# A retuned gather schedule: 0.62 instead of 0.8 row gathers per block during the routing, and the last rows spread to four blocks from the end

## The chip, the cores and the metric

The kernel runs on one core of a Trainium2 chip. The metric is the device time of one execution in microseconds (us); the time of the kernel before is the median of three runs.

## The reference, cut to what matters

One encoder layer: a hyena branch and an RG-LRU branch, mixed into h, then a PEER layer and a final norm. The change lies in the PEER layer, which looks 16,384 single-neuron experts up by product keys and sums the chosen ones:

```
q = (x @ wq).reshape(B, L, PEER_HEADS, 2, D_HALF)
s = jnp.einsum('blhpd,hpkd->blhpk', q, keys)
ts, ti = lax.top_k(s, K)                       # 16 of 128 keys, twice
cs, ci = lax.top_k((ts[..., 0, :, None] + ts[..., 1, None, :]).reshape(...), K)
experts = e1 * N_KEYS + e2                     # 8 heads x 16 experts a token
g = softmax(cs)
act = gelu(einsum('td,tkd->tk', xt, u_tab[et])) * gt
out = einsum('tk,tkd->td', act, v_tab[et])
```

There are 512 tokens, D = 1024, and two expert tables u and v of 16,384 x 1024 float32.

## The kernel before

The PEER layer treats the 512 tokens in two ways. For the first 384 tokens (TD) nothing is gathered: all 128 **blocks** of 128 experts are multiplied through. A u block is 24 matmuls (ps_e) of the block's weights with x2, followed by a gelu on ScalarE (L1019); a v block is 18 matmuls into ob (L1045) with the weights pt = gelu x routing weight. For the last 128 tokens (TG) the rows themselves are gathered from the tables by indirect DMAs that GpSimd issues (L1160), 512 KB each (128 tokens, one row of 4 KB each): 128 gathers from u, each followed by a dot product on VectorE (L1194, called a *dot* below), then 128 from v, each followed by an accumulation on VectorE (L1215).

Every block's weights come as float32 by a DMA on SyncE's queue (wf, L149) and are split into two float16 halves, the high one on ScalarE (L119), the low one on VectorE (L120); four such wh buffers exist, so the splits can run about two blocks ahead of TensorE.

The order of the work is written by one loop over `seq`: 101 u blocks, then 27 pairs of a u and a v block, then v blocks (in the code i counts v blocks, 0 to 127). The instructions of each engine run in the order in which the loop writes them. Three sources feed VectorE:

- the split of the block two ahead;
- until the routing is done, `pull` draws background steps (the **routing**: selecting the experts, and for the 384 tokens building one-hot tiles oh and og, which TensorE multiplies into ps_gt and ScalarE copies to stg, L1369). `pull` adds PACE = 4.2 us of nominal VectorE time a block to a budget and draws steps until it is spent;
- `gathers(rate)`: adds `rate` to a credit gcr and runs one gather step (a dot, or later an accumulation, and the issue of the gather five rows on) for each whole credit. During the routing each step takes 1.3 us from the same budget.

There are 264 gather steps, the last five being `gather_end`: it adds the residual to acc2 by two TensorE results (ps_x, L1224 and L1227) and runs `final` for the last 128 tokens. When the routing is done, the block in which that happens flushes the remaining ps_gt, closes the routing's PSUM pool and opens the one for ob; from then on `gathers` runs at GRATE[1] = 1.5 a block, and from v block i = 32 at a rate that spreads what is left. The last VT = 3 v blocks are held back and multiplied per 128 tokens just before `final`.

The gather steps in the routing and the stages after it:

```
self.pull(*self.PACE)
self.bud[0] -= 1.3 * gathers(self.GRATE[0])
```

Of the kernel before, what the change touches and what calls it, by code (L numbers as in the profile page):

```python
# [66 lines left out]
class Kernel:  # L67
# [813 lines left out]
    def peer(self, acc):  # L881
        nc, tc, a = self.nc, self.tc, self.a
        E0, LV, VT = self.E0, self.LV, self.VT
# [93 lines left out]
        def gload(k, q):  # L977
            if k < 128 // EB:
                b = order[EB * k] // EB
                if b not in gin:  # L980
                    gin[b] = vp.tile([128, NCH, EB, CH], F32, name="gin", bufs=2)
                cs = slice(q * NCH // 4, (q + 1) * NCH // 4)
                nc.sync.dma_start(gin[b][:, cs].rearrange("p c e t -> p c (e t)"),
                                  gd[cs, :, CH * EB * b:CH * EB * (b + 1)].rearrange("c p n -> p c n"))
# [7 lines left out]
        def pmul(i):  # L992
            if i >= 128:
                return
            e = order[i]
            if i % EB in (3, 5, 7, 9):
                gload(i // EB + 1, (i % EB - 3) // 2)
            sload(i + 6)
            f = pf[i] = vp.tile([128, TD], F32, name="pf", bufs=2)
            nc.vector.tensor_tensor(f.rearrange("p (c t) -> p c t", c=NCH),  # L1000
                                    sin[e // 2][:, e % 2, :].rearrange("p (c t) -> p c t", c=NCH),
                                    gin[e // EB][:, :, e % EB, :], OP.mult)

        def phi(i):
            if i < 128:
                pt[i] = vp.tile([128, 2, TD], F16, name="pt", bufs=4)
                nc.scalar.activation(pt[i][:, 0, :], pf[i], AF.Copy)  # L1007

        def plo(i):
            if i < 128:  # L1010
                nc.vector.tensor_tensor(pt[i][:, 1, :], pf.pop(i), pt[i][:, 0, :], OP.subtract)  # L1011

        def gelu(e, ps):
            if e % 2 == 0:
                gs[0] = xp.tile([128, 2, TD], F32, name="gs", bufs=3) if e < E0 else \
                    vp.tile([128, 2, TD], F32, name="hs", tag="sin", bufs=4)
                if e >= E0:
                    sin[e // 2] = gs[0]
            nc.scalar.activation(gs[0][:, e % 2, :], ps[:, :TD], AF.Gelu_apprx_tanh, scale=1.0 / (S_N * S_W))  # L1019
            if e % 2 == 1 and e < E0:  # L1020
                self.dq.append((sd[e // 2], gs[0]))

        def spill():
            while self.dq:
                nc.sync.dma_start(*self.dq.pop(0))  # L1025

        def gathers(rate):
            if self.gidx is None:
                return 0
            self.gcr = min(self.gcr + rate, 2.0)  # L1030
            n = 0
            while self.gcr >= 1.0 and self.gq:
                self.gstep()
                self.gcr -= 1.0
                n += 1
            return n
# [3 lines left out]
        def vmm(tt, w, pp, first, last):  # L1040
            mm = nc.tensor.matmul
            sl = slice(tt * 128, tt * 128 + 128)
            for k, (x, y) in enumerate(((0, 0), (0, 1), (1, 0))):
                for h in range(2):
                    mm(ob[tt][:, h, :], pp[:, x, sl], w[:, y, h * 512:(h + 1) * 512],  # L1045
                       start=first and k == 0, stop=last and k == 2)
# [7 lines left out]
        rate = None  # L1054
        for pos, (kind, e) in enumerate(seq):
            if kind == "u":
                w = self.w_get(u0 + pos)
                spill()
                ps = ups.tile([128, 512], F32, name="ps_e", tag="s", bufs=utag)
                for c in range(8):  # L1060
                    self.mm3(ps[:, :TD], w[:, 0, c * 128:(c + 1) * 128], w[:, 1, c * 128:(c + 1) * 128],
                             x2[:, 0, c, :TD], x2[:, 1, c, :TD], c == 0, c == 7)
                if prev is not None:
                    gelu(*prev)
                prev = (e, ps)
                if vp is None:
                    self.pull(*self.PACE)
                    self.bud[0] -= 1.3 * gathers(self.GRATE[0])
                else:
                    gathers(self.GRATE[1])  # L1070
                if vp is None and (route not in self.bgq or e == E0 - 3):
                    while route in self.bgq:
                        self.pull(1.0, 1.0)
                    gelu(*prev)
                    prev = None
                    spill()
                    rctx.close()
                    sctx.close()
                    vp = ctx.enter_context(tc.tile_pool(name="vp", bufs=1, side="right"))
                    self.po = ups = ctx.enter_context(tc.tile_pool(name="pso", bufs=1, space=PSUM))  # L1080
                    utag = 2
                    ob += [ups.tile([128, 2, 512], F32, name="ob%d" % k, tag="ob%d" % k) for k in range(3)]
                    gload(0, 0)
                    e0 = e
                elif vp is not None and e in (e0 + 1, e0 + 2, e0 + 3):
                    gload(0, e - e0)
                    if e == e0 + 1:
                        nc.vector.tensor_scalar(self.ident, self.ident, S_P * S_V, None, op0=OP.mult)
                continue
            i, vi = vi, vi + 1  # L1090
            if i == 0:
                for k in range(3):
                    pmul(k)
                    if k < 2:
                        phi(k)
                        plo(k)
            phi(i + 2)
            pmul(i + 3)
            if i >= 128 - E0:
                if rate is None:  # L1100
                    rate = (268 - self.gsteps) / (E0 - 5.0)
                gathers(rate)
            else:
                gathers(self.GRATE[1])
            plo(i + 2)
            w = self.w_get(u0 + pos)
            pp = pt.pop(i)
            if i >= 128 - VT:
                wl.append((w, pp))
                continue  # L1110
            for tt in range(3):
                vmm(tt, w, pp, i == 0, False)
            if prev is not None:
                gelu(*prev)
                prev = None
            k = i - (128 - E0) - 20
            if 0 <= k < 24:
                tt, c = divmod(k, 8)
                nc.tensor.matmul(ob[tt][:, c // 4, c % 4 * 128:c % 4 * 128 + 128],  # L1119
                                 acc[:, c, tt * 128:tt * 128 + 128], self.ident,  # L1120
                                 start=False, stop=False, skip_group_check=True)
# [23 lines left out]
    E0 = 96  # L1145
    LV = 5
    PACE = (4.2, 4.2)
    TB = 8
    GRATE = (0.8, 1.5)
    LAG = 2  # L1150
    GB = 6

# [388 lines left out]
```

## Time and profile before

| what | value |
|---|---|
| median of 3 runs | 1673.27 us (1672.91 to 1676.97) |
| the profiled execution's own time | 1672.62 us |
| its span | 1670.8 us, so 1.8 us lie around the span |
| TensorE busy | 1610.5 us (96%) |
| VectorE busy | 1407.0 us (84%) |
| ScalarE busy | 767.9 us (46%) |
| GpSimd busy | 379.6 us (23%) |
| DMA | 435.06 MB, mean 260 GB/s |

The shares are means over stages with different limits. The stages that matter here, by the start of the span: the u blocks begin at 578 us, the routing's part with gathers lies between about 690 and 1002 us, u blocks alone follow to 1052 us, pairs to 1256 us, v blocks alone to 1664 us.

### The profile page before, as it was taken

How to read it: one execution, taken by the hardware profiler on the slowest of the kernel's cores; microseconds unless marked ns; L12 is line 12 of the kernel's file. 1: busy time of each engine (PE TensorE's matmuls, PEld its weight loads, DVE VectorE, ACT ScalarE, POOL GpSimd, SP SyncE). 2: the span in 40 equal slices, each digit the busy share in tenths (PEclk: the TensorE clock that was granted, in tenths of full speed). 3: DMA queues.
4: the chain of work that ended last, by engine and by line, in shares of the span. 5: the costliest groups of instructions: out<-in, count | busy, mean ns of one | idle time of the engine just before them, and what ended most of it. 6: DMA issues, size and time to landing. Idle time of an engine off the chain costs nothing. (4 is left out here: it accounts for less than half of the span.)

```text
span 1670.8 us, 25107 instructions
## 1 busy us (share of the span) xinstructions
PE 1610.5 (96%) x9451; PEld 901.7 (54%) x9451; DVE 1407.0 (84%) x2422; ACT 767.9 (46%) x1055; POOL 379.6 (23%) x357
## 2 busy tenths in 40 slices
PE   7999999899989988999998999999999999999998
PEld 5675666444435554666665665555554445544443
DVE  7736679987756799899999996998889998899975
ACT  5424278984431333444755763433333333333343
POOL 0000000002200000332222223555455333333400
PEclk9999999999999999999999999999999999999999
DMA  5342141229932246887888999999999999999951
GB/s 199 96 155 76 38 140 64 65 69 323 338 137 76 77 135 196 301 289 263 308 321 308 340 359 394 406 401 372 380 376 372 398 398 401 394 370 402 398 209 71
DMA packets 137738, 435.06 MB, mean 260 GB/s; under 512 B 13040, under 2 KB 37872, under 8 KB 134160
## 3 DMA queue, kind: packets, MB, share of 16 engines
q1 hardware_dynamic: 95360, 279.72, 46.4%
q0 software_dynamic: 42256, 153.73, 24.4%
q8 instruction: 74, 1.21, 0.3%
q14 instruction: 48, 0.39, 0.1%
HBM read 377.83 MB, written 55.57 MB: 259 GB/s over the span
## 5 line engine op out<-in xcount | busy, mean ns | idle before, releaser
L1045 PE MATMUL ob<-wh,pt 128*128 128x512 f16 x2304 | 505.9, 379 | 0.9 <-ACT pt L1007 0.9
L120 DVE SCALAR_TENSOR_TENSOR wh<-wf,wh 128x1024 f16<-128x1024 f32 (+1 forms) x324 | 389.8, 1207 | 96.8 <-ACT wh L119 96.5
L119 ACT ACTIVATE wh<-wf 128x1024 f16<-128x1024 f32 (+1 forms) x324 | 336.0, 1039 | 107.4 <-DMA wf<-in_peer_u 35.9
L1045 PEld LDWEIGHTS <-pt 128*128 128x128 f16 x2304 | 225.4, 98 | 264.3 <-ACT pt L1007 1.3
L126 PE MATMUL ps_e<-x,wh 128*128 128x384 f16 x1024 | 335.4, 328 | 16.3 <-DVE wh L120 16.3
L124 PE MATMUL ps_e<-x,wh 128*128 128x384 f16 x1024 | 335.1, 327 | 3.3 <-ACT gs L1019 2.3
L125 PE MATMUL ps_e<-x,wh 128*128 128x384 f16 x1024 | 335.4, 328 | 0.0
L1160 POOL DMA_INDIRECT rows<-in_peer_un,gidx x128 | 190.6, 1489 | 358.9 <-DVE junk L1194 314.8
L1160 POOL DMA_INDIRECT rows<-in_peer_v,gidx x128 | 163.2, 1275 | 235.3 <-DVE acc L1215 211.4
L126 PEld LDWEIGHTS <-wh 128*128 128x128 f16 x1376 | 135.1, 98 | 137.1 <-DVE wh L120 29.4
L125 PEld LDWEIGHTS <-wh 128*128 128x128 f16 x1376 | 135.1, 98 | 110.0 <-issue 6.3
L124 PEld LDWEIGHTS <-wh 128*128 128x128 f16 x1376 | 135.2, 98 | 104.0 <-issue 2.1
L1007 ACT ACTIVATE pt<-pf 128x384 f16<-128x384 f32 x128 | 66.8, 522 | 246.1 <-issue 217.7
L1215 DVE SCALAR_TENSOR_TENSOR acc<-rows,dots,acc 128x1024 f32<-128x1024 f32 x127 | 162.6, 1280 | 0.9
L1194 DVE SCALAR_TENSOR_TENSOR junk<-rows,xn 128x1024 f32<-128x1024 f32 x128 | 156.0, 1219 | 0.9
L331 PE MATMUL ps_p<-n,wh 128*128 128x264 f16 x960 | 112.5, 278 | 1.6 <-DVE wh L120 1.5
L1019 ACT ACTIVATE gs<-ps_e 128x384 f32<-128x384 f32 x96 | 47.0, 489 | 138.2 <-PE ps_e L126 126.1
L331 PEld LDWEIGHTS <-wh 128*128 128x128 f16 x960 | 94.4, 99 | 20.4 <-issue 3.5
L1369 ACT ACTIVATE stg<-ps_gt 128x512 f32<-128x512 f32 x96 | 93.0, 1079 | 19.8 <-PE ps_gt L1362 14.3
L1011 DVE TENSOR_TENSOR pt<-pf,pt 128x384 f16<-128x384 f32 x128 | 71.5, 559 | 12.8 <-ACT pt L1007 11.8
L124 PE MATMUL ps_p<-n,wh 128*128 128x512 f16 x192 | 73.6, 383 | 0.0
L125 PE MATMUL ps_p<-n,wh 128*128 128x512 f16 x192 | 73.4, 382 | 0.0
(288 smaller groups left out, 1922.7 us busy)
## 6 DMA issues: line engine op xcount, KB each, us to landing
wf<-in_peer_u SPq DMA_DIRECT2D x128, 512.0 KB, 5.9
wf<-in_peer_v SPq DMA_DIRECT2D x128, 512.0 KB, 10.6
gd<-stg SPq DMA_DIRECT2D x24, 1024.0 KB, 9.2
gin<-gd SPq DMA_DIRECT2D x32, 768.0 KB, 15.1
wf<-in_w_in SPq DMA_DIRECT2D x44, 512.0 KB, 3.6
sd<-gs SPq DMA_DIRECT2D x48, 384.0 KB, 7.1
sin<-sd SPq DMA_DIRECT2D x48, 384.0 KB, 12.6
pre<-ph POOLq DMA_DIRECT2D x18, 512.0 KB, 5.6
```

The source lines that it names most:

```text
L119: self.nc.scalar.activation(hi, src, AF.Copy, scale=s)
L120: self.nc.vector.scalar_tensor_tensor(lo, src, s, hi, op0=OP.mult, op1=OP.subtract)
L124: mm(ps, lh, rh, start=first, stop=False)
L125: mm(ps, lh, rl, start=False, stop=False)
L126: mm(ps, ll, rh, start=False, stop=last)
L331: nc.tensor.matmul(ps[:, h, :HL], x, n[:, y, c, h * HL:(h + 1) * HL], start=(c == 0 and x is lh and y == 0), stop=(c == 7 and x is ll))
L1011: nc.vector.tensor_tensor(pt[i][:, 1, :], pf.pop(i), pt[i][:, 0, :], OP.subtract)
L1045: mm(ob[tt][:, h, :], pp[:, x, sl], w[:, y, h * 512:(h + 1) * 512], start=first and k == 0, stop=last and k == 2)
L1160: self.nc.gpsimd.indirect_dma_start(out=r, out_offset=None, in_=table, in_offset=bass.IndirectOffsetOnAxis(ap=self.gidx[:, j:j + 1], axis=0))
L1194: nc.vector.scalar_tensor_tensor(junk, rows.pop(0), 1.0, self.xn, op0=OP.mult, op1=OP.mult, accum_out=self.dots[:, j:j + 1])
L1215: nc.vector.scalar_tensor_tensor(acc2, r, d, acc2, op0=OP.mult, op1=OP.add)
L1369: nc.scalar.activation(st[c][:, :, o:o + 4].rearrange("p e t -> p t e"), ps, AF.Copy, scale=S_P / S_G)
```

## The change

Two numbers. GRATE[0], the gather steps admitted per block during the routing, goes from 0.8 to 0.62; the rate of the last part is worked out so that the 264 steps end four blocks later.

```diff
@@ peer
             if i >= 128 - E0:
                 if rate is None:
-                    rate = (268 - self.gsteps) / (E0 - 5.0)
+                    rate = (263 - self.gsteps) / (E0 - 4.0)
                 gathers(rate)
@@ class Kernel
-    GRATE = (0.8, 1.5)
+    GRATE = (0.62, 1.5)
```

Because a gather step takes 1.3 us of the budget from which the routing is drawn, fewer steps let the routing be drawn faster: counted in the programs, the block in which the routing ends is the 86th u block instead of the 90th. Up to the routing's last og VectorE has 36 dots instead of 51 and 64 splits instead of 69, counted from the point where the gathers' indices (gidx) are made. At the third set of transposes ps_r (end of the last selection) TensorE has done 71 u blocks instead of 74, and VectorE has run 26 dots instead of 37 and 139 splits instead of 142, with the same 26 og. At v block 32 the accumulations done are 15 instead of 24; from there to v block 96 they are 78 instead of 77. No instruction is added or removed over the whole program.

VectorE where the routing ends, before (oh and og are the routing's one-hot tiles, junk the dot, wh the split):

```order
L1384 TENSOR_TENSOR oh<-iota,ed 128x2048
L1194 SCALAR_TENSOR_TENSOR junk,dots<-rows,xn 128x1024
L120 SCALAR_TENSOR_TENSOR wh<-wf,wh 128x1024
L1388 TENSOR_TENSOR og<-oh,gd_9113 128x2048
L1384 TENSOR_TENSOR oh<-iota,ed 128x2048
L120 SCALAR_TENSOR_TENSOR wh<-wf,wh 128x1024
L1388 TENSOR_TENSOR og<-oh,gd_9113 128x2048
L1194 SCALAR_TENSOR_TENSOR junk,dots<-rows,xn 128x1024
L120 SCALAR_TENSOR_TENSOR wh<-wf,wh 128x1024
```

The same place in the changed program:

```order
L1384 TENSOR_TENSOR oh<-iota,ed 128x2048
L1388 TENSOR_TENSOR og<-oh,gd_9016 128x2048
L120 SCALAR_TENSOR_TENSOR wh<-wf,wh 128x1024
L1384 TENSOR_TENSOR oh<-iota,ed 128x2048
L1388 TENSOR_TENSOR og<-oh,gd_9016 128x2048
L1384 TENSOR_TENSOR oh<-iota,ed 128x2048
L1388 TENSOR_TENSOR og<-oh,gd_9016 128x2048
L1194 SCALAR_TENSOR_TENSOR junk,dots<-rows,xn 128x1024
L120 SCALAR_TENSOR_TENSOR wh<-wf,wh 128x1024
```

Between two splits now stand more oh and og and fewer dots, so the last og comes four blocks sooner.

ScalarE at the same place, before (stg is the copy of a ps_gt, gs the gelu of a u block):

```order
L1369 ACTIVATE stg<-ps_gt 128x4x128 x2
L119 ACTIVATE wh<-wf 128x1024
L1019 ACTIVATE gs<-ps_e 128x384
L1369 ACTIVATE stg<-ps_gt 128x4x128 x2
L119 ACTIVATE wh<-wf 128x1024
L1019 ACTIVATE gs<-ps_e 128x384
L1369 ACTIVATE stg<-ps_gt 128x4x128 x8
L1019 ACTIVATE gs<-ps_e 128x384
L119 ACTIVATE wh<-wf 128x1024 x2
```

and in the changed program:

```order
L1369 ACTIVATE stg<-ps_gt 128x4x128 x2
L119 ACTIVATE wh<-wf 128x1024
L1019 ACTIVATE gs<-ps_e 128x384
L1369 ACTIVATE stg<-ps_gt 128x4x128 x4
L119 ACTIVATE wh<-wf 128x1024
L1019 ACTIVATE gs<-ps_e 128x384
L1369 ACTIVATE stg<-ps_gt 128x4x128 x6
L1019 ACTIVATE gs<-ps_e 128x384
L119 ACTIVATE wh<-wf 128x1024 x2
```

The last copies were 2 + 8 and are 4 + 6; of the 8 two, of the 6 two belong to the block before, so that the routing's last block leaves six copies in the program before and four in the changed one.

VectorE where `gather_end` stands, before (pf and pt are the steps of a v block, acc the residual's addition, fin the start of `final`):

```order
L1227 SCALAR_TENSOR_TENSOR acc_12040<-ps_x,acc_12040 128x512
L1011 TENSOR_TENSOR pt<-pf,pt 128x384
L120 SCALAR_TENSOR_TENSOR wh<-wf,wh 128x1024
L1000 TENSOR_TENSOR pf<-sin,gin 128x384
L1227 SCALAR_TENSOR_TENSOR acc_12040<-ps_x,acc_12040 128x512
L1011 TENSOR_TENSOR pt<-pf,pt 128x384
L120 SCALAR_TENSOR_TENSOR wh<-wf,wh 128x1024
L1000 TENSOR_TENSOR pf<-sin,gin 128x384
L1135 TENSOR_SCALAR fin<-fin 128x1
```

and in the changed program:

```order
L1227 SCALAR_TENSOR_TENSOR acc_12220<-ps_x,acc_12220 128x512
L1011 TENSOR_TENSOR pt<-pf,pt 128x384
L120 SCALAR_TENSOR_TENSOR wh<-wf,wh 128x1024
L1227 SCALAR_TENSOR_TENSOR acc_12220<-ps_x,acc_12220 128x512
L1011 TENSOR_TENSOR pt<-pf,pt 128x384
L120 SCALAR_TENSOR_TENSOR wh<-wf,wh 128x1024
L1135 TENSOR_SCALAR fin<-fin 128x1
```

In the changed program the second addition stands ahead of the very last pt and wh (v block 127) and no pf is left after it; before, seven more pt followed.

## Rows read from the trace of the kernel before

**Rows 1.** The page: the span, and busy time of each engine with its share and instructions.

```profile
span 1670.8 us, 25107 instructions
PE 1610.5 (96%) x9451; PEld 901.7 (54%) x9451; DVE 1407.0 (84%) x2422; ACT 767.9 (46%) x1055; POOL 379.6 (23%) x357
```

**Rows 2.** Busy time by stretch of the routing and of what follows it. Columns: stretch in us, its length, busy us of each engine (instructions), granted TensorE clock, busy share of the DMA engines, GB/s.

```profile
690.00:1002.00 312.00, 302.46 (x2329) 196.16 (x2328) 308.59 (x504) 180.60 (x235) 85.76 (x51) 0.99 0.87 308
...
780.00:911.00 131.00, 124.46 (x976) 80.31 (x974) 129.69 (x211) 76.10 (x99) 36.57 (x22) 1.00 0.87 306
911.00:925.00 14.00, 12.01 (x88) 7.51 (x86) 13.76 (x19) 9.67 (x15) 3.79 (x3) 0.88 0.83 281
925.00:996.00 71.00, 70.26 (x611) 48.17 (x609) 70.56 (x74) 50.45 (x63) 18.92 (x12) 1.00 0.98 359
996.00:1012.40 16.40, 12.83 (x101) 8.13 (x98) 10.77 (x14) 9.47 (x11) 4.00 (x3) 0.90 1.02 405
...
1043.60:1061.40 17.80, 15.89 (x91) 8.70 (x90) 14.15 (x22) 6.67 (x10) 8.54 (x6) 1.00 1.03 416
1061.40:1256.00 194.60, 194.60 (x1051) 102.72 (x1050) 174.96 (x239) 74.81 (x105) 104.36 (x76) 1.00 1.01 384
```

**Rows 3.** The same view of the last part, v blocks alone.

```profile
1300.00:1400.00 100.00, 100.00 (x474) 47.13 (x472) 91.77 (x107) 37.30 (x51) 37.92 (x31) 1.00 1.04 399
1400.00:1500.00 100.00, 100.00 (x480) 48.35 (x478) 90.81 (x105) 36.74 (x50) 35.34 (x30) 1.00 1.02 385
1500.00:1600.00 100.00, 100.00 (x466) 45.30 (x464) 93.44 (x108) 37.25 (x52) 35.00 (x28) 1.00 1.01 392
```

**Rows 4.** What TensorE waited for between 690 and 1010 us: total us, times, longest.

```profile
PE ps_e L126 <- DVE wh L120: 5.3, 8, 1.0
PE ps_gt L1362 <- ACT stg L1369: 3.3, 9, 0.8
PE ps_e L124 <- ACT gs L1019: 2.3, 1, 2.3
PE ps_gt L1362 <- DVE og L1388: 1.9, 2, 1.2
```

**Rows 5.** What VectorE waited for in the same stretch (the only row), and below it its two groups that the change moves, 690 to 1002 us: line, engine, operation, tiles, shapes, count, busy us, mean ns, idle before.

```profile
DVE wh L120 <- ACT wh L119: 5.6, 1, 5.6
...
L120 DVE SCALAR_TENSOR_TENSOR wh<-wf,wh 128x1024 f16<-128x1024 f32 x65 | 79.2, 1220 | 0.0
L1194 DVE SCALAR_TENSOR_TENSOR junk<-rows,xn 128x1024 f32<-128x1024 f32 x52 | 63.3, 1216 | 0.0
```

**Rows 6.** Matmuls of u blocks (tile ps_e) over ten blocks that wait for nothing: 240 matmuls in 39 us.

```profile
687.50:726.50 39.00, 38.84 (x240) 4.90 (x10) 1.00 0.79 268
```

**Rows 7.** VectorE in order of time before the routing's end: start us, us, what; in brackets idle time before it.

```profile
994.08 1.22 DVE L1194 SCALAR_TENSOR_TENSOR junk<-rows,xn 128x1024 f32<-128x1024 f32 x1
...
995.22 1.22 DVE L120 SCALAR_TENSOR_TENSOR wh<-wf,wh 128x1024 f16<-128x1024 f32 x1
...
996.36 1.22 DVE L1388 TENSOR_TENSOR og<-oh,gd 128x2048 f16<-128x2048 f16 x1
...
999.77 1.22 DVE L1388 TENSOR_TENSOR og<-oh,gd 128x2048 f16<-128x2048 f16 x1
```

**Rows 8.** TensorE and ScalarE in order of time where the routing ends.

```profile
995.12 1.06 PE L1362 MATMUL ps_gt<-og,oh 128*128 128x128 f16 x16
...
999.91 1.50 PE L1362 MATMUL ps_gt<-og,oh 128*128 128x128 f16 x24
1000.56 1.96 ACT L1369 ACTIVATE stg<-ps_gt 128x512 f32<-128x512 f32 x2 [2.85 <-PE ps_gt L1362]
...
1002.84 3.60 ACT L1369 ACTIVATE stg<-ps_gt 128x512 f32<-128x512 f32 x4 [0.32 <-DMA gd<-stg]
...
1006.24 0.52 ACT L1019 ACTIVATE gs<-ps_e 128x384 f32<-128x384 f32 x1
...
1006.80 0.32 PE L124 MATMUL ps_e<-x,wh 128*128 128x384 f16 x1 [2.28 <-ACT gs L1019]
...
1008.11 0.52 PE L124 MATMUL ps_e<-x,wh 128*128 128x384 f16 x1
1008.43 0.52 PE L125 MATMUL ps_e<-x,wh 128*128 128x384 f16 x1
...
1011.40 0.33 PE L124 MATMUL ps_e<-x,wh 128*128 128x384 f16 x1
1011.57 0.33 PE L125 MATMUL ps_e<-x,wh 128*128 128x384 f16 x1
```

**Rows 9.** Busy time by stretch, as in rows 2, where the granted clock falls.

```profile
916.00:920.00 4.00, 2.54 (x22) 1.67 (x23) 3.97 (x4) 4.00 (x8) 0.30 (x1) 0.83 0.95 357
...
1008.00:1011.00 3.00, 3.00 (x11) 1.41 (x10) 2.96 (x4) 0.64 (x1) 0.64 (x1) 0.53 1.03 430
```

**Rows 10.** Waits between 1006 and 1062 us, after the routing: SyncE's queue, ScalarE, TensorE.

```profile
SPq L983 <- DMA gd<-stg: 9.2, 1, 9.2
...
ACT wh L119 <- DMA wf<-in_peer_u: 11.7, 3, 4.6
...
PE ps_e L124 <- ACT hs L1019: 1.0, 1, 1.0
PE ob L1045 <- ACT pt L1007: 0.9, 1, 0.9
```

**Rows 11.** TensorE and VectorE at `gather_end`, in order of time.

```profile
1618.77 1.05 PE L1224 MATMUL ps_x<-ident,xt 128*128 128x128 f32 x8
...
1619.86 0.69 DVE L1227 SCALAR_TENSOR_TENSOR acc<-ps_x,acc 128x512 f32<-128x512 f32 x1 [5.42 <-PE ps_x L1224]
...
1624.63 0.69 DVE L1227 SCALAR_TENSOR_TENSOR acc<-ps_x,acc 128x512 f32<-128x512 f32 x1 [2.02 <-PE ps_x L1224]
1625.24 0.55 DVE L1011 TENSOR_TENSOR pt<-pf,pt 128x384 f16<-128x384 f32 x1
```

## The prediction

> **What bounds the kernel now.** I read the page first: TensorE is busy 96% of the span, so almost everything that a schedule can win is TensorE's idle time, some 60 us in all [rows 1]. Then the busy time by stretch, to see where that idle time lies in the part that the change touches. From 1061 us on TensorE never stops, through the pairs [rows 2] and the v blocks alone [rows 3]; nothing can be won there, only lost. In the routing, 690 to 1002 us, it stands idle for 9.5 us of 312, and 6.5 of these lie between 780 and 911 us, 2.0 between 911 and 925, 0.7 between 925 and 996 [rows 2]. Where the routing ends, 3.6 us more are idle within 16.4, and 1.9 us where the first v block starts, between 1043.6 and 1061.4 [rows 2]. That is the whole purse: about 15 us.
>
> Who is waited for? TensorE's waits in the routing name VectorE's split first (eight waits, 5.3 us), then ScalarE's copies of ps_gt (3.3), one gelu (2.3), VectorE's og (1.9) [rows 4]. VectorE itself waits for nothing until the routing's end, where it waits once, 5.6 us for ScalarE [rows 5]; its instructions follow each other without a gap, a dot, a split, an og each starting 1.14 us after the one before [rows 7] (the 1.22 of the groups overlaps by 0.08). So in the routing VectorE is the slower queue by a little. TensorE started with splits done well ahead, used that lead up by 780 us, and then meets late splits until about 911 us. After 925 us each block carries ps_gt work, TensorE is the slower one again, and the lead comes back.
>
> **The change, part by part.** Prices: a u block that waits for nothing takes 3.9 us (240 matmuls, 24 a block, in 39 us) [rows 6]. A dot or a split is 1.14 us of VectorE [rows 7]. Eight matmuls of ps_gt are 0.44 us, from 1.50 us for 24 and 1.06 for 16 [rows 8].
>
> *The routing up to the last selection.* VectorE loses 15 dots and 5 splits ahead of the last og, 20 x 1.14 = 22.8 us, and TensorE has 4 x 3.9 = 15.6 us fewer in front of the same place. The four blocks still have to be run afterwards, so the most that can come of it is 22.8 - 15.6 = 7.2 us, if TensorE hung on VectorE to the end. It doesn't: after 925 us it is busy 70.26 of 71 us [rows 2], and what VectorE saves there is not paid out. The place up to which it does hang is the third ps_r, which stands at 915 us, in the stretch 911 to 925. Up to there the change takes out 11 dots and 3 splits, 14 x 1.14 = 16.0 us, and 3 blocks, 11.7 us, of TensorE: 4.3 us net. Not all of that arrives. The first 33 blocks hold two dots fewer (2.3 us) and no block fewer; TensorE waits for nothing there, so VectorE only gets further ahead, and with four wh buffers it can't keep a lead beyond about two blocks. I take off 1.5 us of the 2.3 as lost in this way, an estimate between 0 and 2.3. **2.7 us gained**, with bounds 0 (the late splits are local and come back in another block) and 7.2.
>
> *The routing's end.* From the end of the last routing block's own matmuls (999.91) to the next block's first (1006.80) pass 6.9 us, in which six groups of ps_gt (2.6 us) are done: 4.3 us lost. ScalarE sets this time: six copies one after the other, then the gelu, for which the first block after the routing waits [rows 8]. The changed order leaves four copies there; two copies fewer are 2 x 0.9 = 1.8 us (3.60 us for four) [rows 8], two groups fewer are 0.9 us of TensorE's work that moves one block forward: 0.9 us net. That earlier block now has four groups where there are three ps_gt buffers, which costs a wait like the nine that make up 3.3 us [rows 4], 0.4 us. **0.5 us gained**, bounds 0 and 2.
>
> *Four more u blocks at 1.5 gathers each.* They fall between the routing's end and the first v block. TensorE lost 1.9 us there: 1.0 behind a gelu that stood in ScalarE's queue behind weights that came late, 0.9 for the first pt [rows 10]. The late weights come from SyncE's queue, where the loads of gin wait 9.2 us for the last gd write to land, with the wf loads behind them [rows 10]. That delay moves along with the routing's end. The first pt, though, is now made four blocks (15.6 us) further from the gin loads. I take about half of the 1.9 us as saved: **0.5 us gained**, bounds 1.9 gained and 5 lost (the four blocks each as slow as 5.1 us, 1.2 us over 3.9; worked out from 1.9 + 3 x 0.9 as the nearest idle time).
>
> *The last part.* At v block 32 nine accumulations are still to be done that were done before. They spread over the blocks to four from the end: 78 instead of 77 in the 64 blocks up to block 96, the rest behind block 115, where before no gather work was left. VectorE is busy 91 to 93% there and TensorE 100% [rows 3]; one accumulation in 64 blocks changes nothing. **0**, covered by VectorE's free 7%. If the cover were gone, nine accumulations, each at the 1.2 us of a dot [rows 5], 10.9 us, would stand on the path.
>
> *The tail.* VectorE waits 5.4 and 2.0 us for TensorE to reach the two ps_x [rows 11]. Before, eight blocks lay behind it; now only the split and pt of block 127 stand behind the second. From the first ps_x TensorE has a block (18 matmuls, 3.9 us at 466 in 100 us [rows 3]), a ps_x of 1.05 us and two blocks' share of six matmuls each ahead, 2.6 us, together 7.5 us [rows 11]; VectorE waits about 5 us for the second ps_x, then takes 0.6 for the addition (1624.63 to 1625.24), 0.5 for pt and 1.14 for the split, 7.2 us. It fits by a hair: **0**, bound 1 lost. The last rows' `final` ends while the first of the three others starts.
>
> Sum: 2.7 + 0.5 + 0.5 = 3.7 us. The profiled execution took 1672.62 us, so 1668.9; the median of the runs shown lies 0.65 above it, so **1669.6 us**. About 0.3% (5.0 us) is what a measurement of this kernel can tell from no change, so I forecast a gain that falls just inside that.
>
> **The rivals.** *The clock comes back as well (1666 to 1668 us).* Twice here the granted clock falls to the lower level, 1.2 GHz: in 916 to 920 us it is 0.83 on the mean, in 1008 to 1011 us 0.53 [rows 9], each time behind a stretch in which TensorE was often idle; matmuls of u blocks then start 0.32 us apart instead of 0.16 [rows 8]. A stretch of some 3.4 us (1008.0 to 1011.4) at half speed costs 1.7 us. Fewer late splits and a shorter stop could spare one (3.7 + 1.7 = 5.4 us gained, 1667.9) or both (7.1 us, 1666.2). Against it: the stop at the routing's end gets shorter by a quarter only. The Trainium skill, "TensorE: Matmul & The Clock Gate", section "What's actually happening", says that the clock has two levels and that idleness throttles it; the trace agrees, with 0.53 behind the stop of 2.28 us.
>
> *Nothing moves (1671 to 1675 us).* The stalls between 780 and 911 us could be local: a block with 7.4 us of background stalls whatever the mean. For it speaks that each wait is at most 1.0 us [rows 4]; against it that the waits begin only when VectorE's lead is used up.
>
> *The transfers bind after the routing (1675 to 1682 us).* The change takes 15 rows of 0.524 MB and four blocks' weights, 7.9 + 2.1 MB, out of a stretch that moves 308 GB/s at a busy share of 0.87 and puts them behind it, where 384 to 416 GB/s run at 1.0 and more [rows 2, 3]. Were that part paced by the DMA engines, 10.0 MB at 392 GB/s would take 25.5 us, and the routing ends only 15.6 + 3.2 = 18.8 us sooner: 6.7 us net lost, 1680. It decides from where that part, at 384 to 399 GB/s now, asks for more than the engines give. Against it: TensorE stands still nowhere behind 1061 us, and 416 GB/s were reached between 1043.6 and 1061.4 [rows 2], so 6% are free. The Trainium skill, "DMA: Bandwidth & Descriptors", section "Where 436 GB/s comes from", holds that the HBM side binds at about 358 GB/s for a core; by that rule the later part would be full already and 4.7 MB more there (nine rows) would cost 13 us. The trace doesn't agree: 399 GB/s over 100 us with TensorE at 100% [rows 3].
>
> **How the numbers follow.** The forecast (2 to 5 us gained) gets 0.44; the clock too, or more of the 7.2 us, 0.38; nothing moves 0.06; transfers 0.12. So faster by over 0.3%: 0.38; within: 0.50; slower: 0.12. The range takes in both clock stretches and most of the bound of 7.2 us below (1664.5), and the first of the losses above (1674.5); the forecast's own is 1667.5 to 1671.5.
>
> **What would show it.** Right: the routing's last ps_gt some 19 us sooner; TensorE's waits for the split below 4 us in the routing; VectorE still without gaps up to the third ps_r; four copies in the stop at the routing's end, and about 5 us from its last matmul to the next block; no TensorE idle time from the pairs to the end. Wrong: waits of TensorE for pt or wh behind 1200 us (transfers or VectorE bind), late weights for longer than two blocks behind the routing, a stop at the second ps_x, or a changed count of stretches at the lower clock.

## The result: slower, by a wait for one write behind the gin loads

The changed kernel takes 1683.09 us, the median of four runs (1680.80 to 1684.03), against 1673.09 of the kernel before on the same chip: a ratio of 1.0057, with a 95% interval of 1.0045 to 1.0070. The prediction was 1669.6 us, in a range of 1664.5 to 1674.5. The time lies 8.6 us above that range, and on the other side of the kernel before.

The profiled execution took 1682.42 us. Its page, to be held against [rows 1]:

```profile
span 1680.6 us, 25104 instructions
PE 1613.3 (96%) x9451; PEld 903.5 (54%) x9451; DVE 1408.2 (84%) x2422; ACT 767.4 (46%) x1055; POOL 383.1 (23%) x357
```

TensorE's busy time rose by only 2.8 us while the span rose by 9.8. So TensorE stands still longer, and the question is where. The busy time by stretch of the changed kernel, with the columns of [rows 2] and nearly the same bounds (the stretch from 925 to 996 us is divided at 970):

```profile
780.00:911.00 131.00, 125.25 (x1005) 82.23 (x1004) 129.59 (x209) 82.43 (x108) 26.90 (x16) 1.00 0.83 291
...
925.00:970.00 45.00, 42.73 (x362) 29.10 (x362) 43.39 (x43) 33.32 (x41) 7.95 (x5) 0.96 0.94 341
970.00:996.00 26.00, 23.13 (x194) 15.49 (x193) 20.76 (x24) 16.65 (x21) 6.58 (x5) 0.93 0.90 328
996.00:1012.40 16.40, 16.40 (x103) 9.87 (x102) 12.70 (x19) 6.23 (x9) 8.39 (x7) 1.00 1.02 400
1012.40:1043.60 31.20, 21.22 (x114) 11.83 (x113) 14.28 (x20) 6.80 (x9) 10.36 (x8) 0.84 1.04 392
...
1300.00:1400.00 100.00, 100.00 (x472) 46.76 (x471) 92.96 (x108) 37.24 (x52) 38.78 (x31) 1.00 1.04 398
```

Between 1012.4 and 1043.6 us TensorE does nothing for 10.0 us, and the mean granted clock is 0.84. In the kernel before it was busy throughout there, with the DMA engines at the same share and rate:

```profile
1012.40:1043.60 31.20, 31.20 (x194) 18.79 (x193) 20.69 (x29) 10.54 (x15) 13.42 (x11) 1.00 1.04 390
```

By the starts of the blocks, counted from u block 0:

| from, to | before | changed |
|---|---|---|
| u block 24 to u block 92 | 328.8 us | 327.3 us |
| u block 92 to the first v block | 41.2 us | 51.9 us |
| first v block to the end of the span | 613.3 us | 613.3 us |

The routing gained 1.5 us, the last part and the tail nothing, and the stretch between the routing and the pairs lost 10.7; 0.6 us of difference lies ahead of u block 24, before the change begins. Together that is the span's 9.8 us. The 10.7 can be read block by block: u block 93 takes 14.0 us instead of 3.9 (10.1 lost), u block 94 takes 6.7 (2.8 lost), and the two places where the kernel before had its 1.9 us of idle time are free of it (2.2 saved).

What ended the wait? TensorE's, ScalarE's and SyncE's waits in that stretch (total us, times, longest; TensorE from 1010 to 1062 us, the other two from 980 to 1045):

```profile
PE ps_e L124 <- ACT gs L1019: 10.0, 1, 10.0
...
ACT gs L1019 <- DMA sd<-gs: 11.1, 1, 11.1
ACT wh L119 <- DMA wf<-in_peer_u: 6.8, 2, 4.6
...
SPq L983 <- DMA gd<-stg: 12.7, 1, 12.7
```

TensorE waits for a gelu, the gelu for a DMA that writes gs to sd, and SyncE's queue was held for 12.7 us by the last gd write. (sd and gd lie in DRAM: sd takes the gelus of the u blocks below 96, gd the routing's weights from stg; gin is what is read back of gd for the v blocks.) How the three hang together is seen in the order of SyncE's queue (start us, length, what is issued):

```profile
990.41 0.44 SPq L1025 DMA_DIRECT2D sd<-gs  x1
1003.68 0.38 SPq L983 DMA_DIRECT2D gin<-gd  x1
...
1008.71 5.33 SPq L149 DMA_DIRECT2D wf<-in_peer_u  x1
1014.08 0.44 SPq L983 DMA_DIRECT2D gin<-gd  x1
1014.62 7.16 SPq L149 DMA_DIRECT2D wf<-in_peer_u  x1
1021.82 0.43 SPq L1025 DMA_DIRECT2D sd<-gs  x1
```

A gelu of a u block below 96 goes to a gs tile, of which there are three; two blocks share one, and sd is the DMA that frees it. The routing now ends in the 86th block. The pair 86/87 (blocks counted from 0) is therefore the first whose sd stands behind the gin loads. The first of these waits for the last gd write (990.9 to 1003.7). From there the four gin loads and the four wf loads between them take another 18.1 us to issue; two of the wf loads hold the queue for 5.3 and 7.2 us. What these two wait for is not shown: a wf buffer comes round with every sixth load, and VectorE's splits that emptied the two in question had ended at 998.9 and 1002.7. So the write of 86/87 is issued at 1021.82. Pairs 88/89 and 90/91 take the two tiles left, and the gelu of block 92 wants the tile of 86/87:

```profile
1020.70 1.06 ACT L119 ACTIVATE wh<-wf 128x1024 f16<-128x1024 f32 x1 [4.59 <-DMA wf<-in_peer_u]
...
1032.81 0.49 ACT L1019 ACTIVATE gs<-ps_e 128x384 f32<-128x384 f32 x1 [11.06 <-DMA sd<-gs]
```

This is ScalarE; the bracket is its idle time and what ended it. The write landed some 11 us after its issue, and block 94 on TensorE, whose PSUM is what that gelu empties, started at 1033.36.

In the kernel before the same rule does no harm, because the routing ended in the 90th block. The sd of the last pair before the gin loads was issued ahead of them, the pairs 90/91, 92/93 and 94/95 take the three tiles once each, and from block 96 the gelus go to hs tiles, which need no write. Its queue, for comparison:

```profile
1006.88 0.43 SPq L1025 DMA_DIRECT2D sd<-gs  x1
...
1016.68 0.38 SPq L983 DMA_DIRECT2D gin<-gd  x1
...
1022.82 7.21 SPq L983 DMA_DIRECT2D gin<-gd  x1
...
1034.51 0.44 SPq L1025 DMA_DIRECT2D sd<-gs  x1
```

There the next sd is just as late, 17.8 us behind the first gin load (18.1 in the changed kernel), and nobody waits for it. The longest hold, 7.2 us, falls on a gin load there, for which no split has to free anything.

The clock did the rest. The stretches of the changed kernel from 700 to 1600 us in which the granted clock was at its lower level, 1.2 GHz (columns as above; the 0.50 is the clock):

```profile
926.40:929.80 3.40, 3.32 (x16) 1.98 (x16) 3.37 (x4) 3.40 (x6) 0.00 (x0) 0.50 1.02 419
991.20:994.60 3.40, 3.40 (x13) 1.58 (x12) 3.34 (x5) 0.97 (x2) 0.70 (x1) 0.50 1.01 421
1028.80:1039.00 10.20, 5.64 (x18) 2.60 (x18) 4.68 (x7) 2.76 (x4) 1.68 (x1) 0.50 1.03 418
```

The third begins within the 10 us stop, and TensorE then works for 5.6 us at half speed; that is the 2.8 us of block 94. The first two are the two of the kernel before, 3.4 us long there as well, in the routing and behind the stop at its end ([rows 9] show parts of them, with means of 0.83 and 0.53).

### The profile page after: what moved, and what is told of

Its sections match the earlier page's. It is cut to its first block, busy times and chain, and to the rows that moved or that the text cites. A ratio compares the mean times of both kernels' runs of the same rounds, so it can differ in the third digit from the quotient of the medians.

```text
span 1680.6 us, 25104 instructions
## 1 busy us (share of the span) xinstructions
PE 1613.3 (96%) x9451; PEld 903.5 (54%) x9451; DVE 1408.2 (84%) x2422; ACT 767.4 (46%) x1055; POOL 383.1 (23%) x357
## 5 line engine op out<-in xcount | busy, mean ns | idle before, releaser
L126 PE MATMUL ps_e<-x,wh 128*128 128x384 f16 x1024 | 336.3, 328 | 15.6 <-DVE wh L120 15.4
L125 PEld LDWEIGHTS <-wh 128*128 128x128 f16 x1376 | 135.4, 98 | 119.0 <-issue 15.6
```

The costliest lines, as they stand in the source:

```text
L125: mm(ps, lh, rl, start=False, stop=False)
L126: mm(ps, ll, rh, start=False, stop=last)
```

## The experiments

Three theories were held against each other. **The tile:** the gelu of block 92 reuses a gs tile whose write is late, because the routing ends four blocks earlier. **The transfers:** the work pushed behind the routing is paced by the DMA engines, as in the prediction's third rival. **The last part:** the changed rate costs time at the end. Each ratio below is against the kernel before on the same chip. A difference in us between two variants is one of their medians, also where they ran on different chips; on these the kernel before took 1672.39 to 1673.53 us.

### Each half of the change alone

The changed kernel with the old rate of the last part:

```diff
-                    rate = (263 - self.gsteps) / (E0 - 4.0)
+                    rate = (268 - self.gsteps) / (E0 - 5.0)
```

> Only the routing's rate changes (0.62), the last part's rate formula is that of the kernel before. Theory A (a buffer: the gelu of u block 92 must wait until the sd write of blocks 86 and 87 has left one of three gs tiles, and that write stands in SyncE's queue behind the loads of gin): the one wait of about 10 us stays, 1681 to 1684 us, 0.5 to 0.7% over the kernel before. Theory B (more transfers behind the routing bind, spread over the later stages): also about 1682, with the loss in many places. Theory C (the new end of the gathers costs at the tail): 1671 to 1674.

Measured: 1682.67 us, ratio 1.0058 (1.0040 to 1.0075). TensorE's wait for gs is there again, 10.7 us long.

The kernel before with only the new rate of the last part (the same line, the other way round):

> Only the last part's rate formula changes, the routing keeps 0.8. Theory A and theory B: nothing to be seen, 1672 to 1674 us, ratio 0.999 to 1.001. Theory C (the end of the gathers costs): 1680 or more.

Measured: 1672.70 us, ratio 1.0000 (0.9991 to 1.0010). The whole loss belongs to GRATE[0], and the last part costs nothing.

### Two more gs tiles

The changed kernel; the gelus of 92/93 and 94/95 get tiles of their own, in the space of two that are no longer used (tv and ti, which get a tag for it; those two lines are left out below). No DMA, no order and no rate is touched.

```diff
...
-                gs[0] = xp.tile([128, 2, TD], F32, name="gs", bufs=3) if e < E0 else \
+                gs[0] = xp.tile([128, 2, TD], F32, name="gs", bufs=3) if e < 92 else \
+                    xp.tile([128, 2, TD], F32, name="gx", tag="tv" if e == 92 else "ti", bufs=1) if e < E0 else \
```

> The whole change; the gelus of u blocks 92, 93 and of 94, 95 go into two other buffers (the slots of tv and ti, which nothing reads any more at that time) instead of two of the three gs tiles. All DMAs, their queue and their order stay. Theory A1 (the wait is for the gs buffer): the wait of 10 us is gone, the late weights of some 4 us (they were hidden behind it) remain, 1671 to 1676 us. Theory A2 (SyncE's queue as a whole is late there, the buffer only shows it): 1680 or more.

Measured: 1673.07 us, ratio 0.9999 (0.9990 to 1.0009); 10.0 us less than the changed kernel. TensorE's and ScalarE's waits from 985 to 1070 us (the new tiles are gx; lines stand one lower than in the changed kernel):

```profile
PE ps_e L124 <- ACT gx L1020: 2.4, 2, 2.0
...
ACT wh L119 <- DMA wf<-in_peer_u: 23.3, 10, 5.4
```

The stop of 10.0 us is down to 2.4, for weights that come late in the same stretch. That settles the tile as the cause: the writes still stand behind the gin loads in SyncE's queue, and the DMA engines have the same bytes to move in the same order. By blocks, u block 92 to the first v block takes 41.9 us in this profile, 10.0 less than in the changed kernel. The run also shows that the gain forecast did not appear once this obstacle was gone: the kernel is then equal to the one before. TensorE's and ScalarE's waits inside its routing, 690 to 985 us:

```profile
ACT stg L1370 <- DMA gd<-stg: 12.6, 4, 7.3
...
PE ps_gt L1363 <- ACT stg L1370: 6.9, 5, 5.8
```

A write to gd was late there once by 7.3 us, and TensorE lost 5.8 for it; in the changed kernel's own profile its longest wait of this kind is 2.2 us. This is the second thing that the prediction had not seen: the writes of the routing stand in the same queue as everything else.

### The threshold: a rate of 0.75

The changed kernel with GRATE[0] = 0.75 in place of 0.62. The routing ends in the 89th block, one earlier than before; fewer rows move than by 0.62.

> The change with 0.75 in place of 0.62: the routing ends in the 89th u block, one sooner than in the kernel before. Theory A: from this block on one pair of u blocks more needs a gs buffer whose write stands behind the loads of gin (blocks 94, 95 on the buffer of 88, 89), so nearly the whole wait appears at one block's shift: 1678 to 1683 us. Theory B (bytes moved behind the routing): three or four rows moved instead of fifteen, 1674 to 1676.

Measured: 1683.41 us, ratio 1.0057 (1.0041 to 1.0073). TensorE's waits for stg from 690 to 985 us, and what it and ScalarE wait for from 985 to 1070:

```profile
PE ps_gt L1362 <- ACT stg L1369: 10.2, 8, 6.1
...
PE ps_e L124 <- ACT gs L1019: 10.2, 2, 7.9
...
ACT gs L1019 <- DMA sd<-gs: 13.7, 1, 13.7
```

One block of shift costs as much time as four. With the routing's end in the 89th block, the pair 88/89 is the first behind the gin loads, the pairs 90/91 and 92/93 take the other two tiles, and 94/95 comes back to the first. Not all of the loss is the tile's, though. In this profile TensorE's wait for the tile is 7.9 us (the other 2.3 are the stop at the routing's end), and u block 92 to the first v block takes 48.8 us, 7.6 more than before; another 4.6 us are lost inside the routing, where TensorE waits 6.1 us once for a stg copy. So one block brings 7.6 of the 10.7 us that four bring. A loss that was paced by bytes would have grown with the number of rows moved, fifteen by 0.62 and three or four here.

### The writes on ScalarE's queue, and gin later

The changed kernel; the writes of gs and stg (sd and gd) are issued from ScalarE's queue:

```diff
-                nc.sync.dma_start(*self.dq.pop(0))
+                nc.scalar.dma_start(*self.dq.pop(0))
```

> The whole change, with the writes of gs and stg (sd and gd) issued from ScalarE's queue instead of SyncE's, so that none stands behind the loads of gin. Theory A: the wait of 10 us for the sd write is gone and so is the stretch at the lower clock behind it, some 12 us; 1668 to 1673 us. Theory B (bandwidth): the same bytes in the same stretch, 1679 or more.

Measured: 1670.99 us, ratio 0.9993 (0.9983 to 1.0002). That is 11.7 us less than the changed kernel alone with its old last rate, on the same chip. What is left from 985 to 1062 us:

```profile
PE ps_e L124 <- ACT gs L1019: 4.4, 2, 4.2
...
ACT wh L119 <- DMA wf<-in_peer_u: 15.7, 5, 6.0
```

The wait for sd is gone; a gelu is late by 4.2 us because it stands in ScalarE's queue behind splits of weights that came late, and in the end behind the issue of a write. The weights come late behind the gin loads, which still stand in SyncE's queue. The Trainium skill, "DMA: Bandwidth & Descriptors", section "Issuing engines are not separate DMA queues", says that starting DMAs from several engines saves only the time that the sequencer takes to start them. Here the same bytes on the same 16 engines became 11.7 us cheaper: what was saved was the waiting of one DMA behind another in the order of its issuing queue.

The other way round, the writes left on SyncE's queue, and the four gin loads moved from the blocks e0 to e0 + 3 to the blocks e0 + 3 to e0 + 6 (e0 is the block in which the routing ends):

```diff
-                    gload(0, 0)
...
-                elif vp is not None and e in (e0 + 1, e0 + 2, e0 + 3):
-                    gload(0, e - e0)
+                elif vp is not None and e0 < e <= e0 + 6:
+                    if e >= e0 + 3:
+                        gload(0, e - e0 - 3)
```

> The whole change, with the four first loads of gin issued three blocks later, when the last gd write has landed, so that SyncE's queue is not held at the first of them for 12.7 us and the sd write of blocks 86 and 87 stands ahead of most of them. Theory A: the wait of 10 us is gone, 1668 to 1673 us. Theory B: 1679 or more, as the transfers are the same.

Measured: 1675.91 us, ratio 1.0021 (1.0009 to 1.0032). The expectation was missed: only part of the loss came back. SyncE's issue of the write of 86/87, and the gelu that waits for it, in this kernel:

```profile
1006.24 2.15 SPq L1025 DMA_DIRECT2D sd<-gs  x1
...
1026.20 0.49 ACT L1019 ACTIVATE gs<-ps_e 128x384 f32<-128x384 f32 x1 [10.16 <-DMA sd<-gs]
```

The write is issued 15.6 us sooner than in the changed kernel, but lands only just before 1026.2, some 20 us later, where it had taken 11. TensorE still waits 4.4 us for a gelu. An early issue was not enough. Behind it in the same queue are the gin loads and the weights; why its landing took 20 us no run here takes apart.

Both edits together:

> The whole change, with sd and gd issued from ScalarE's queue and the loads of gin three blocks later. If what is left in the version with ScalarE's queue alone (4.2 us behind weights that are late because SyncE's queue is held by the first gin load) is such a wait, it goes: 1665 to 1669 us. If the weights are late from bandwidth, 1670 to 1672.

Measured: 1668.26 us, ratio 0.9973 (0.9965 to 0.9982). From ScalarE's queue a write of gs lands in 7 us; the first line is the issue of the four writes between 1000 and 1045 us, the second the time to their landing:

```profile
L1025 ACTq DMA_DIRECT2D sd<-gs x4: 326/326/326, 1003.4 to 1034.5; - x4
...
DMA to landing us min/median/max: 6.8/7.1/7.6
```

This place in the queue has a price too: here ScalarE stood idle for 7.9 us, put down to a weight load that had not landed, before it issued one of these writes and ran the gelu behind it, and TensorE lost 2.2 us.

With two more gs tiles on top of these edits:

> Both edits on the change, and the two other buffers for the gelus of blocks 92 to 95. If no gs wait is left once sd has its own queue, the same as without them, 1667 to 1669 us; if the gs buffers still cost, 1664 to 1667.

Measured: 1669.37 us, ratio 0.9979 (0.9970 to 0.9989), 0.4 us above the range expected. The tiles, worth 10 us in the changed kernel, are worth nothing here: as soon as the write has left SyncE's queue, no gelu waits for a tile.

### The same edits without the faster routing

The kernel before with the writes on ScalarE's queue, and with both edits:

> The kernel before (0.8, old last rate) with sd and gd issued from ScalarE's queue. Theory A: no wait for sd exists there, so little moves, 1670 to 1674 us; what it gains is to be taken off what the same edit gains on the change.

> The kernel before (0.8, old last rate) with both edits that helped the change: sd and gd from ScalarE's queue, gin three blocks later. If the gain of these edits over the kernel before (0.27%) is theirs alone, the same here: 1667 to 1669 us. If it needs the change's faster routing, 1671 to 1676, as with the first edit alone.

Measured: 1675.07 us, ratio 1.0012 (1.0004 to 1.0021), and 1673.56 us, ratio 1.0006 (0.9997 to 1.0015). The first is slower: TensorE waits 3.3 us for one gelu behind weights that come late, and then runs 5.5 us at the lower clock, which costs another 2.8. So the queue by itself is no gain. What the edits give, they give by letting the faster routing through: the lower rate with both edits stands 5.3 us below the same edits with the old rate (1668.26 and 1673.56).

### How far the rate can go

Both edits, with GRATE[0] = 0.5 (the routing ends in the 84th block) and 0.4 (in the 82nd):

> Both edits on the change with 0.5 instead of 0.62, so that the routing ends in the 84th block instead of the 86th. If VectorE's queue is still what TensorE waits for in the routing, 1 to 3 us less than with 0.62: 1665 to 1667. If the u blocks alone are then the slow part (late weights, DMA at its limit), no gain or a loss: 1668 to 1674.

> Both edits on the change with 0.4, so that the routing ends in the 82nd block; 0.5 gave 1664.2 us and 0.62 gave 1668.3. If VectorE's queue still holds TensorE up in the routing, another 1 to 3 us less, 1661 to 1663. If the purse of late splits is empty and the u blocks alone (now 19 of them at 1.5 gathers) or the last part take the gain back, 1664 to 1668.

Measured: **1664.20 us, ratio 0.9949 (0.9935 to 0.9963)** at 0.5, the lowest median of all, 18.9 us below the changed kernel and 0.8 below what was expected; and 1667.09 us, ratio 0.9966 (0.9955 to 0.9977) at 0.4. TensorE's waits from 690 to 960 us at 0.5:

```profile
PE ps_gt L1362 <- ACT stg L1369: 4.2, 9, 2.2
PE ps_r L1331 <- DVE sm_w L1322: 1.1, 1, 1.1
```

and at 0.4:

```profile
PE ps_gt L1362 <- ACT stg L1369: 4.9, 10, 1.4
PE ps_gt L1362 <- DVE og L1388: 1.7, 2, 1.1
```

At either rate no split is late any more, the term that the prediction was after; only the routing's own chain is left. At 0.4 nothing more was won there: TensorE waits 1.3 us longer in the same 270 us. From u block 24 to the first v block the two profiles differ by 2.0 us (361.6 and 363.6), and TensorE is busy 100% from 1060 to 1600 us in both. That covers their difference of 1.7 us in profiled time. The medians differ by 2.9, but they are from two chips, on which the kernel before took 1672.39 and 1673.53, and the intervals of the two ratios overlap: that 0.4 is worse than 0.5 is not shown.

## Why the prediction was wrong, by its own steps

**The step that failed is the third, four more u blocks at 1.5 gathers each.** It put 0.5 us of gain there, with bounds of 1.9 gained and 5 lost, and the profile shows 10.7 lost. It had the right row: SyncE's queue waits 9.2 us for gd, with the loads behind it [rows 10]. It asked only what the wf loads behind that wait would do, and said that the delay "moves along with the routing's end". It never asked what else stands in that queue and who needs it: sd writes, which free the gs tiles. In the kernel before they were late by the same 18 us without being needed. Four blocks sooner, the three tiles run out. The trace of before showed that resource too: between 840 and 880 us two gelus wait for an sd write to land (ScalarE's row):

```profile
ACT gs L1019 <- DMA sd<-gs: 4.1, 2, 2.1
```

And the code shows how much of it there is: three tiles, two blocks each, from the routing's end to block 96. That is 6 blocks before, starting at block 90, and 10 after. Had the working counted the reuses, the price was at hand in the trace of before. There the seventh gelu behind the routing's end is the first that goes to an hs tile (ScalarE, in order of time):

```profile
1036.46 0.47 ACT L1019 ACTIVATE hs<-ps_e 128x384 f32<-128x384 f32 x1
```

and the write of the pair 90/91, issued at 1034.51, lands so long after its issue (the last number, us):

```profile
sd<-gs SPq DMA_DIRECT2D x1, 384.0 KB, 13.5
```

So it landed at about 1048.0. A seventh gelu that needed its tile would have waited some 11.6 us, an estimate from these rows alone; in the changed kernel it does need it, and waited 11.1.

The saving which this step did forecast exists, and is larger than the 0.5 us it was given: 2.2 us, since the gelu behind late weights and the first pt no longer wait. It was swamped by 10.1 of waiting and 2.8 at the lower clock.

**The routing up to the last selection (2.7 us): right.** From the start of u block 24 to the third ps_r TensorE takes 212.8 us in the changed kernel (second line), 227.5 before:

```profile
687.50:914.98 227.48, 220.94 (x1623) 140.43 (x1622) 224.44 (x432) 120.46 (x160) 62.57 (x38) 1.00 0.84 293
...
688.10:900.92 212.82, 208.57 (x1553) 133.75 (x1550) 207.84 (x405) 117.87 (x156) 43.71 (x26) 1.00 0.80 279
```

That is 14.7 us less, of which 11.7 are the three u blocks that now come later: 3.0 gained. The sign that was named for it failed all the same: late splits are still 4.5 us in the routing, not below 4.

**From the last selection to the stop at the routing's end (put at nothing): too hopeful.** The prediction had no term here, since TensorE was busy 70.26 of 71 us. From the third ps_r to the first block behind the routing the changed kernel takes 89.4 us and the kernel before 91.8 with one u block more (3.9): 1.5 lost, although the stop, with the 0.5 us forecast for it, is in this piece. So of the 3.2 us that the first two steps promised, 1.5 arrived. What TensorE waits for between 690 and 1010 us, to be held against [rows 4], one row of VectorE (690 to 986) and one of ScalarE (690 to 1010):

```profile
PE ps_e L126 <- DVE wh L120: 4.5, 6, 1.1
PE ps_gt L1362 <- ACT stg L1369: 3.6, 6, 2.2
PE ps_e L124 <- ACT gs L1019: 2.3, 1, 2.3
PE ps_gt L1362 <- DVE og L1388: 1.4, 2, 1.0
...
DVE wh L120 <- ACT wh L119: 2.0, 1, 2.0
...
ACT stg L1369 <- DMA gd<-stg: 9.5, 5, 4.4
```

VectorE waits for ScalarE only once there, so it is still the slower of the two. But ScalarE waits 9.5 us for gd writes to free its stg tiles, 5.5 before: fed faster, the routing runs into its own writes. With the writes on ScalarE's queue and gin later no such wait is left, and the same piece takes 85.4 us, 4.0 less than in the changed kernel; 2.3 of that is idle time, and 1.7 the clock, which did not fall within it there. In that kernel u blocks 24 to 92 took 323.3 us, 5.5 less than before, and 321.4 at a rate of 0.5, 7.4 less. So the bound of 7.2 us was of the right size, but it took moving the writes off SyncE's queue to come near it, and part of it is the clock, which the term did not count.

**The stop at the routing's end: right.** TensorE there (the next block is the last line):

```profile
985.67 1.50 PE L1362 MATMUL ps_gt<-og,oh 128*128 128x128 f16 x24
...
990.34 0.32 PE L124 MATMUL ps_e<-x,wh 128*128 128x384 f16 x1 [2.28 <-ACT gs L1019]
```

From 985.67, where [rows 8] give 999.91, to the next block pass 4.7 us; about 5 were forecast, and 6.9 stood there before. The place lies 16.5 us sooner by the next block (1006.80 before), not some 19, since the piece in front of it was slower.

**The last part and the tail (0 and 0): right.** TensorE is at 100% of 100 us [rows 3 and the table of stretches above], and the first v block to the end takes 613.3 us in both. VectorE's two waits for ps_x, 5.42 and 2.0 in [rows 11]:

```profile
1656.86 0.69 DVE L1227 SCALAR_TENSOR_TENSOR acc<-ps_x,acc 128x512 f32<-128x512 f32 x1 [5.42 <-PE ps_x L1224]
...
1661.63 0.69 DVE L1227 SCALAR_TENSOR_TENSOR acc<-ps_x,acc 128x512 f32<-128x512 f32 x1 [2.48 <-PE ps_x L1224]
```

The second wait is 2.48 us, where the working had about 5; TensorE waits for nothing there.

**The rivals.** "The transfers bind" came nearest in place and number (1675 to 1682, 1680 worked out), but its mechanism is not the one: one block's shift brings most of the loss, two more tiles take it away with the same transfers, and where TensorE stops the DMA engines move 392 GB/s, as they did before (390) with TensorE busy throughout. A forecast that is near for another reason is no confirmation. "The clock comes back" went the other way: both stretches at the lower level are still there, and a third, three times as long, came with the longer stop. The signs that the prediction had named for itself being wrong included "late weights for longer than two blocks behind the routing"; the stop came a step further on, from late writes.

## What to carry to other kernels

When a change moves a stage's end, list everything that stands in the issuing queue behind the DMA that waits there, writes too, and for each ask which buffer it frees and how many uses later that buffer is wanted again: a queue that is late by 18 us before and after can be free of charge with three tiles for three pairs, and cost 13 us with three tiles for five. Stalls of this kind are thresholds, not slopes, so a small step of a tuning number can bring most of the price (7.6 of 10.7 us by one block here). And a scheduling number that looks exhausted may be held by a queue: the rate alone lost 0.6%, the queue edits alone gained nothing, and both together gained 0.3%, and 0.5% with the rate at 0.5.

## What the runs showed of the hardware that was not expected

A write of 384 KB that is issued early need not land early: in the queue shared with the gin loads and the weights it took about 20 us with gin moved back and about 11 us in the changed kernel, and 7 us from ScalarE's queue, at a DMA share of 1.0 or more around all of them. Issuing can be slow as well: with the same share, single loads held SyncE's queue for 5.3 to 7.2 us, although the buffers they write had been free for 6 us and more. And the granted clock fell to its lower level with stops of very different length: for 3.4 us behind the routing's end with its wait of 2.28 us, and for 10.2 us with one of 10.0 us.
